# FFN gate and up kept in PSUM, and x transposed once, in a one-core hybrid decoder step

## The chip, the cores and the metric

The kernel runs on one core of a Trainium2 chip. The metric is the device time of one execution in microseconds (us). A core has five engines with a queue each, and every queue runs in order: PE (TensorE, matrix products and transposes; PEld is its weight load), DVE (VectorE), ACT (ScalarE), POOL (GpSimd) and SP, which here only issues DMAs. PE, DVE and ACT can work on PSUM, eight banks of 2 KB in each partition, into which PE writes; SBUF is the main on-chip memory.

## The reference

One inference step of a two-layer decoder, for one prompt of 512 tokens and for 8 requests of 4 tokens each, so 544 columns in all, with 1024 features. Layer 0 mixes with gated DeltaNet, layer 1 with sparse attention; each is followed by a SwiGLU FFN with 2816 hidden features. What the change touches is this part of it:

```python
def rmsnorm(x, w):
    xf = x.astype(jnp.float32)
    y = xf * lax.rsqrt(jnp.mean(xf * xf, axis=-1, keepdims=True) + NORM_EPS)
    return y.astype(x.dtype) * w

def swiglu_ffn(h, w_in, w_out):
    gate, up = jnp.split(h @ w_in, 2, axis=-1)
    return (jax.nn.silu(gate) * up) @ w_out

# run_trunk, layer l
h = rmsnorm(x, P['norm_mix'][l])
...
x = x + y
x = x + swiglu_ffn(rmsnorm(x, P['norm_ffn'][l]), P['ffn_w_in'][l], P['ffn_w_out'][l])
```

## The kernel before

Activations lie transposed: features on the 128 partitions, the 544 columns (512 prompt, 32 sample) along the free axis, in 8 blocks of 128 features. Every fp32 product is made of three matmuls: each weight tile and each activation tile is split into a rounded high part and a low part (the rest), and `gemm` (L171) issues hi*hi (L177), hi*lo (L178) and lo*hi (L179) for each of the 8 blocks. The 544 columns go in two halves, of 256 and of 288. `load_w` (L161) fetches 128 weight columns of all 8 blocks as one 128x1024 tile, ACT makes the high part `whi` (L158) and DVE, or POOL where `pool_lo` is set, the low part `wlo = wraw - whi` (L159). There are two buffers each of `whi` and `wlo`.

`start` (L227) brings x in. Five row tiles `xt` (tokens on partitions) are squared and summed, DVE and POOL make 1/rms per token in `col`, and for each half PE transposes all tiles to `raw`, which goes back to DRAM as the residual (L277, L278, L284). Then the row tiles are multiplied by their token's 1/rms (L289 on POOL, L291 on DVE), PE transposes them a second time (L300), and `make_u` (L211) takes each transposed block out of PSUM: ACT writes the high part times the norm weight `nv` (L213), DVE the low part (L214). The transposed norm weights come from one tile `vr` of 41 rows, filled by four DMAs (L294, L295). The products that follow are the decay gates (16 weight columns) and then the q, k, v projections of the DeltaNet.

`ffn` (L936) goes through 22 hidden blocks j in two groups of 11. For each j it loads a gate and an up weight tile, and for each half makes gate `pg` in a `mm` bank and up `pu` in an `aux` bank (four banks of each), 24 matmuls each. Then DVE scales gate into SBUF tile `fa` (L967), ACT takes tanh into `fth` (L968), DVE scales up into `fup` (L969), forms (1+tanh)*gate in `fth` (L970) and the hidden value in `fup` (L971), ACT rounds it to `hh` (L972), and DVE writes the rest to `hl` (L973). After 11 blocks `proj_add` multiplies by the second FFN matrix. Beside the first half of layer 0's FFN runs `past_blocks` (L1060): POOL gathers cached rows by indirect DMAs and multiplies and adds 128x512 tiles in SBUF (L1089, L1091). Layer 1's FFN has no POOL work beside it.

A scheduler puts the instructions in order on each engine when the program is built, from its own estimate of durations; on the chip each queue then runs that order.

Of the kernel before, what the change touches and what calls it, by code (L numbers as in the profile page):

```python
# [10 lines left out]
F32 = mybir.dt.float32  # L11
# [3 lines left out]
AF = mybir.ActivationFunctionType  # L15
OP = mybir.AluOpType
# [95 lines left out]
class Net:  # L112
# [114 lines left out]
    def start(self, up, hist):  # L227

        A, T, V, S, G = self.A, self.T, self.V, self.S, self.G
# [11 lines left out]
        with self.tc.tile_pool(name="xin", bufs=1) as xp:  # L241
            vr = xp.tile([48, 128], F32, name="vr")
# [9 lines left out]
            self.dma(vr[32:40], A["norm_kv"].rearrange("(k p) -> k p", p=128))  # L252
            self.dma(vr[40:41], A["dn_out_norm"])
            self.dma(cr, A["dn_conv_w"].rearrange("l i (c p) -> (l i c) p", p=128))
            self.load_consts()
            for half, (c0, cn) in enumerate(HALVES):
# [28 lines left out]
                for q in range(2):  # L285
                    for i, (t, n, _) in enumerate(tiles):
                        x = xt[t][0:n, q * 512:(q + 1) * 512]
                        if i == 1:
                            G.tensor_scalar(x, x, col[0:n, i:i + 1], 1.0, op0=OP.mult, op1=OP.mult)  # L289
                        else:  # L290
                            V.tensor_scalar(x, x, col[0:n, i:i + 1], None, op0=OP.mult)  # L291
                if half == 0:
                    ps = self.bank(next(bank))
                    T.transpose(ps[:, 0:41], vr[0:41], ident[0:41, 0:41])  # L294
                    V.tensor_copy(self.nv, ps[:, 0:41])  # L295
                    V.tensor_scalar(self.nvh, self.nv[:, 40:41], 0.5, None, op0=OP.mult)
                for k in range(KD):
                    ps = self.bank(next(bank))[:, 0:cn]
                    for t, n, o in tiles:
                        T.transpose(ps[:, o:o + n], xt[t][0:n, k * 128:(k + 1) * 128], ident[0:n, 0:n])  # L300
                    self.make_u(ps, self.nv[:, k:k + 1], *[t[:, c0:c0 + cn] for t in u[k]])

            ps = self.aux()
            T.transpose(ps[:, 0:96], cr, ident[0:96, 0:96])
            V.tensor_scalar(self.cw, ps[:, 0:96], 0.5, None, op0=OP.mult)
            for g in range(3):
# [629 lines left out]
    def ffn(self, l, u, after, side=(), steps=0):  # L936
# [5 lines left out]
        with self.tc.tile_pool(name="ffn", bufs=1) as hp, self.tc.tile_pool(name="ffs", bufs=2) as fs:  # L942
            for j0, jn in ((0, 11), (11, 11)):
                hid = []
                for j in range(j0, j0 + jn):
# [12 lines left out]
                    for c0, cn in HALVES:  # L958
# [7 lines left out]
                        a, th, up = [fs.tile([128, 288], F32, name=n)[:, :cn] for n in ("fa", "fth", "fup")]  # L966
                        V.tensor_tensor(a, pg, rstd[:, cs], op=OP.mult)  # L967
                        S.activation(th, a, AF.Tanh, scale=0.5)  # L968
                        V.scalar_tensor_tensor(up, pu, 0.5, rstd[:, cs], op0=OP.mult, op1=OP.mult)  # L969
# [847 lines left out]
```

## Time and profile before

| What | Value |
|---|---|
| median of 3 runs | 1655.19 us (1652.71 to 1656.19) |
| profiled execution | 1663.51 us |
| its span (first to last instruction) | 1661.7 us |
| mean granted TensorE clock | 0.985 of full |
| PE busy | 1598.3 us, 96% |
| DVE busy | 1062.2 us, 64% |
| ACT busy | 709.8 us, 43% |
| POOL busy | 564.5 us, 34% |

The profile is of one execution, which took 8.3 us more than the median of the runs. A busy PE in it is one with a matmul in its pipeline; a slot in which no matmul runs, or in which the granted clock is lower, lowers the count of matmuls in a stretch. In a row of a timeline the first number is the start, the second the duration, and brackets hold the engine's idle time before the instruction and who ended it. Back-to-back instructions overlap a little, so the distance of two starts is shorter than a duration.

### The profile page before, as it was taken

Reading aid. Unit: us, or ns where it says so; the run is one execution under the profiler, and the core shown is the slowest. Engines: PE = TensorE matmul, PEld = TensorE weight load, DVE = VectorE, ACT = ScalarE, POOL = GpSimd, SP = SyncE. Lnnn points to the kernel's source line nnn. Section 1 sums busy time; section 2 is a strip of 40 time slices with the busy share of each in tenths; the row PEclk is TensorE's granted clock in tenths of the full one; section 3 lists DMA queues with packets and bytes.
Section 4 is the critical chain, followed back from the end, with each engine's and each line's share of the span. In section 5 each row is a group of like instructions: output and inputs, shape, how many; then the busy total and the mean of one; then the engine's idle time right before and its main releaser. Section 6 shows DMA issues by size and latency. Waiting matters only on the chain.

```text
span 1661.7 us, 32748 instructions
## 1 busy us (share of the span) xinstructions
PE 1598.3 (96%) x12527; PEld 1528.5 (92%) x12527; DVE 1062.2 (64%) x2543; ACT 709.8 (43%) x1796; POOL 564.5 (34%) x861
## 2 busy tenths in 40 slices
PE   8998898998989999999999999999999999999997
PEld 7998788987989999999999999877999999999997
DVE  5879779487577753555556688678875553355533
ACT  5554554553323222232332487778843232132233
POOL 3675546424366711100145476565520000000000
PEclk9999999999999999999999999999999999999999
DMA  6233412257556634354342532523133332334222
GB/s 195 77 78 93 109 36 70 72 163 219 138 143 142 160 101 117 95 164 132 108 140 81 147 95 78 177 70 112 45 96 102 102 106 79 108 90 127 77 88 81
DMA packets 289069, 183.37 MB, mean 110 GB/s; under 512 B 25183, under 2 KB 271784, under 8 KB 288784
## 3 DMA queue, kind: packets, MB, share of 16 engines
q1 hardware_dynamic: 286352, 172.88, 37.5%
q0 software_dynamic: 2560, 8.39, 1.4%
q8 instruction: 99, 1.62, 0.4%
q14 instruction: 58, 0.48, 0.1%
HBM read 159.33 MB, written 26.90 MB: 112 GB/s over the span
## 4 chain that ended last, share of the span: by engine, by line
PE 77%; DVE 10%; POOL 4%; DMA 3%; ACT 3%; issue 2%; SPq 0%; POOLq 0%; DVEq 0%; ACTq 0%
PE mm L179 15%; PE mm L177 15%; PE mm L178 15%; PE aux L177 5%; PE aux L178 5%; PE aux L179 5%; PE po L1641 2%; PE aux L1668 2%; DVE hb L595 2%; DVE hb L597 1%; DVE wlo L159 1%; PE mm L1578 1%; PE mm L1579 1%; PE mm L818 1%; DVE cy L470 1%
## 5 line engine op out<-in xcount | busy, mean ns | idle before, releaser
L177 PE MATMUL mm<-uh,whi 128*128 128x288 f32 (+2 forms) x1824 | 531.3, 293 | 5.1 <-DVE hb L689 1.7
L179 PE MATMUL mm<-uh,wlo 128*128 128x288 f32 (+2 forms) x1824 | 523.8, 292 | 6.7 <-DVE wlo L159 6.7
L178 PE MATMUL mm<-ul,whi 128*128 128x288 f32 (+2 forms) x1824 | 530.1, 292 | 0.0
L158 ACT CAST whi<-wraw 128x1024 fp32r<-128x1024 f32 (+5 forms) x231 | 215.9, 936 | 524.0 <-PE mm L178 431.0
L177 PEld LDWEIGHTS mm<-uh,whi 128*128 128x128 f32 (+1 forms) x1824 | 343.9, 189 | 8.4 <-DVE hb L689 2.1
L179 PEld LDWEIGHTS mm<-uh,wlo 128*128 128x128 f32 (+1 forms) x1824 | 341.0, 189 | 9.2 <-DVE wlo L159 8.3
L178 PEld LDWEIGHTS mm<-ul,whi 128*128 128x128 f32 (+1 forms) x1824 | 344.3, 189 | 1.5 <-issue 0.4
L159 DVE TENSOR_TENSOR wlo<-wraw,whi 128x1024 fp32r<-128x1024 f32 (+5 forms) x207 | 235.5, 1138 | 118.6 <-ACT whi L158 117.2
L179 PE MATMUL aux<-uh,wlo 128*128 128x288 f32 (+1 forms) x704 | 202.7, 288 | 3.1 <-DVE wlo L159 3.1
L177 PE MATMUL aux<-uh,whi 128*128 128x288 f32 (+1 forms) x704 | 203.3, 289 | 0.0
L178 PE MATMUL aux<-ul,whi 128*128 128x288 f32 (+1 forms) x704 | 203.3, 289 | 0.0
L177 PE MATMUL mm<-hh,whi 128*128 128x256 f32 (+1 forms) x704 | 202.0, 289 | 0.0
L178 PE MATMUL mm<-hl,whi 128*128 128x256 f32 (+1 forms) x704 | 201.4, 288 | 0.0
L179 PE MATMUL mm<-hh,wlo 128*128 128x256 f32 (+1 forms) x704 | 196.5, 288 | 0.0
L179 PEld LDWEIGHTS aux<-uh,wlo 128*128 128x128 f32 x704 | 133.1, 189 | 3.6 <-DVE wlo L159 3.6
L184 POOL TENSOR_TENSOR ycol<-yvar,nhalf 128x2 f32<-128x2 f32 (+1 forms) x2 | 1.6, 775 | 390.2 <-DVE yvar L1716 390.2
L178 PEld LDWEIGHTS aux<-ul,whi 128*128 128x128 f32 x704 | 133.1, 189 | 0.0
L177 PEld LDWEIGHTS aux<-uh,whi 128*128 128x128 f32 x704 | 132.8, 189 | 0.2 <-issue 0.2
L178 PEld LDWEIGHTS mm<-hl,whi 128*128 128x128 f32 x704 | 132.6, 188 | 0.0
L177 PEld LDWEIGHTS mm<-hh,whi 128*128 128x128 f32 x704 | 132.6, 188 | 0.0
L179 PEld LDWEIGHTS mm<-hh,wlo 128*128 128x128 f32 x704 | 129.6, 188 | 0.0
L969 DVE SCALAR_TENSOR_TENSOR fup<-aux,rstd 128x256 f32<-128x256 f32 x88 | 38.6, 439 | 122.9 <-PE aux L179 122.9
(535 smaller groups left out, 2969.1 us busy)
## 6 DMA issues: line engine op xcount, KB each, us to landing
wraw<-in_ffn_w_in_dram SPq DMA_DIRECT2D x88, 512.0 KB
wraw<-in_dn_w_in_dram SPq DMA_DIRECT2D x32, 512.0 KB
wraw<-in_ffn_w_out_dram SPq DMA_DIRECT2D x32, 384.0 KB
wraw<-in_ffn_w_out_dram SPq DMA_DIRECT2D x32, 320.0 KB
hb<-in_state_dn_S_dram SPq DMA_DIRECT2D x32, 256.0 KB
wraw<-in_nsa_w_kv_dram SPq DMA_DIRECT2D x12, 512.0 KB
bskew<-bscr SPq DMA_DIRECT2D x16, 320.0 KB
x<-xd SPq DMA_DIRECT2D x16, 272.0 KB
```

The source lines that it names most:

```text
L158: self.S.copy(hi, src)
L159: (self.G if pool_lo else self.V).tensor_tensor(lo, src, hi.bitcast(F32), op=OP.subtract)
L177: self.T.matmul(ps, lhsT=hi[:, k, :], rhs=uh[:, cs], start=first and k == 0, stop=False)
L178: self.T.matmul(ps, lhsT=hi[:, k, :], rhs=ul[:, cs], start=False, stop=False)
L179: self.T.matmul(ps, lhsT=lo[:, k, :], rhs=uh[:, cs], start=False, stop=last and k == kc - 1)
L470: V.scalar_tensor_tensor(y[:, 0:SEQ], pre[:, i:i + SEQ], cw[i], y[:, 0:SEQ], op0=OP.mult, op1=OP.add)
L595: V.tensor_tensor(t, D[a][:, 0:m, l:l + 1].to_broadcast([64, m, n]), row.to_broadcast([64, m, n]), op=OP.mult)
L597: V.tensor_tensor(N[a][:, 0:m, l:32], N[a][:, 0:m, l:32], t, op=OP.subtract)
L818: T.matmul(ps, lhsT=Kh, rhs=um[q], start=True, stop=True)
L969: V.scalar_tensor_tensor(up, pu, 0.5, rstd[:, cs], op0=OP.mult, op1=OP.mult)
L1641: T.matmul(self.po, lhsT=self.VT[ty][:, kb, g], rhs=m[:, i:i + 2].rearrange("p e q -> p (e q)"), start=False, stop=last and kb > k0 and m ...
L1668: T.transpose(ps[:, i * 128:(i + 1) * 128], P[2 * pr + e][ty][:, a:a + 128], ident)
```

## The change

In `start` the second transpose is gone. 1/rms of each token is spread over all partitions by one transpose of a broadcast column (`rep`), and the block of x already transposed in `raw` (SBUF) is multiplied with it: on even blocks by one DVE instruction that also multiplies by the norm weight, followed by `split`; on odd blocks by POOL, followed by `make_u`. The norm weights needed first get a tile of their own with 32 rows; the other nine rows are transposed later. In `ffn` tanh is written into the gate's PSUM bank, up is scaled in its own bank, the product overwrites that bank, and `hh` and `hl` are made from there; only `fa` stays in SBUF. The low parts of the weights stay where they were.

```diff
-            vr = xp.tile([48, 128], F32, name="vr")
+            vr = xp.tile([32, 128], F32, name="vr")
+            vr2 = xp.tile([16, 128], F32, name="vr2")
...
-                for q in range(2):
-                    for i, (t, n, _) in enumerate(tiles):
-                        x = xt[t][0:n, q * 512:(q + 1) * 512]
-                        if i == 1:
-                            G.tensor_scalar(x, x, col[0:n, i:i + 1], 1.0, op0=OP.mult, op1=OP.mult)
-                        else:
-                            V.tensor_scalar(x, x, col[0:n, i:i + 1], None, op0=OP.mult)
                 if half == 0:
                     ps = self.bank(next(bank))
-                    T.transpose(ps[:, 0:41], vr[0:41], ident[0:41, 0:41])
-                    V.tensor_copy(self.nv, ps[:, 0:41])
-                    V.tensor_scalar(self.nvh, self.nv[:, 40:41], 0.5, None, op0=OP.mult)
+                    T.transpose(ps[:, 0:32], vr, ident[0:32, 0:32])
+                    V.tensor_copy(self.nv[:, 0:32], ps[:, 0:32])
+
+                ps = self.bank(next(bank))
+                for i, (t, n, o) in enumerate(tiles):
+                    T.transpose(ps[:, o:o + n], col[0:n, i:i + 1].to_broadcast([n, 128]), ident[0:n, 0:n])
+                rep = xp.tile([128, cn], F32, name=f"rep{half}")
+                V.tensor_copy(rep, ps[:, 0:cn])
                 for k in range(KD):
-                    ps = self.bank(next(bank))[:, 0:cn]
-                    for t, n, o in tiles:
-                        T.transpose(ps[:, o:o + n], xt[t][0:n, k * 128:(k + 1) * 128], ident[0:n, 0:n])
-                    self.make_u(ps, self.nv[:, k:k + 1], *[t[:, c0:c0 + cn] for t in u[k]])
+                    x = xp.tile([128, cn], F32, name=f"xn{half}", bufs=3)
+                    if k % 2:
+                        G.tensor_tensor(x, raw[:, k], rep, op=OP.mult)
+                        self.make_u(x, self.nv[:, k:k + 1], *[t[:, c0:c0 + cn] for t in u[k]])
+                    else:
+                        V.scalar_tensor_tensor(x, raw[:, k], self.nv[:, k:k + 1], rep, op0=OP.mult, op1=OP.mult)
+                        self.split(*[t[:, c0:c0 + cn] for t in u[k]], x)
...
-                        a, th, up = [fs.tile([128, 288], F32, name=n)[:, :cn] for n in ("fa", "fth", "fup")]
+
+                        a = fs.tile([128, 288], F32, name="fa")[:, :cn]
                         V.tensor_tensor(a, pg, rstd[:, cs], op=OP.mult)
-                        S.activation(th, a, AF.Tanh, scale=0.5)
-                        V.scalar_tensor_tensor(up, pu, 0.5, rstd[:, cs], op0=OP.mult, op1=OP.mult)
-                        V.scalar_tensor_tensor(th, th, 1.0, a, op0=OP.add, op1=OP.mult)
-                        V.tensor_tensor(up, th, up, op=OP.mult)
-                        S.copy(hh[:, cs], up)
-                        V.tensor_tensor(hl[:, cs], up, hh[:, cs].bitcast(F32), op=OP.subtract)
+                        S.activation(pg, a, AF.Tanh, scale=0.5)
+                        V.scalar_tensor_tensor(pu, pu, 0.5, rstd[:, cs], op0=OP.mult, op1=OP.mult)
+                        V.scalar_tensor_tensor(a, pg, 1.0, a, op0=OP.add, op1=OP.mult)
+                        V.tensor_tensor(pu, pu, a, op=OP.mult)
+                        S.copy(hh[:, cs], pu)
+                        V.tensor_tensor(hl[:, cs], pu, hh[:, cs].bitcast(F32), op=OP.subtract)
```

Behind `start` all engines keep the order of before, apart from a few neighbours that change places. In `start` itself the order on PE differs most. Before, the first product of the program (16 columns, the decay gates) follows the second transposes (L300) of the first half, and the second half's first transposes (L277) come behind it:

```order
L300 MATMUL ch<-ct,xt_155 128x128
L300 MATMUL ch<-ct,xt_156 128x128
L177 MATMUL mm<-uh,whi 16x256
L178 MATMUL mm<-ul,whi 16x256
L300 MATMUL ch<-ct,xt_155 128x128
L300 MATMUL ch<-ct,xt_156 128x128
L277 MATMUL aux<-ct,xt_157 128x128
```

Now it follows the transposes of both halves (L278 and L283 of the changed file), and the row of the second half's 1/rms (L293) comes right behind it:

```order
L278 MATMUL ch<-ct,xt_158 128x128
L278 MATMUL ch<-ct,xt_159 128x128
L283 MATMUL ch<-ct,xt_160 128x32 x8
L177 MATMUL mm<-uh,whi 16x256
L178 MATMUL mm<-ul,whi 16x256
L293 MATMUL aux<-ct,xcol 128x128 x2
L293 MATMUL aux<-ct,xcol 128x32
```

So PE now has all of x transposed before the first product, and ACT copies the second half's `raw` ahead of the first half's high parts. On DVE, at the same place, before: each low part is one instruction (L214) whose x operand is a PSUM bank.

```order
L187 SCALAR_TENSOR_TENSOR xcol<-rs_w,xcol 128x2
L291 TENSOR_SCALAR xt_155<-xt_155,xcol 128x512 x2
L266 SCALAR_TENSOR_TENSOR sq,xss<-xt_158 128x1024
L295 COPY nv<-ch 128x41
L270 TENSOR_SCALAR xss<-xss 128x3
L296 TENSOR_SCALAR nvh<-nv 128x1
L214 SCALAR_TENSOR_TENSOR ul<-aux,nv,uh 128x256
L214 SCALAR_TENSOR_TENSOR ul<-ch,nv,uh 128x256
```

Now (L302 is the product of an even block, L159 and L214 the low parts, `xn` the SBUF tile between):

```order
L187 SCALAR_TENSOR_TENSOR xcol<-rs_w,xcol 128x2
L267 SCALAR_TENSOR_TENSOR sq,xss<-xt_159 128x1024
L295 COPY rep_216<-aux 128x256
L302 SCALAR_TENSOR_TENSOR xn_218<-raw_184,nv,rep_216 128x256
L302 SCALAR_TENSOR_TENSOR xn_226<-raw_184,nv,rep_216 128x256
L271 TENSOR_SCALAR xss<-xss 128x3
L185 SCALAR_TENSOR_TENSOR rs_w<-xcol 128x3
L186 TENSOR_TENSOR rs_w<-rs_w,xss 128x3
L159 TENSOR_TENSOR ul<-xn_218,uh 128x256
L187 SCALAR_TENSOR_TENSOR xcol<-rs_w,xcol 128x3
L159 TENSOR_TENSOR wlo<-wraw,whi 128x8x16
L214 SCALAR_TENSOR_TENSOR ul<-xn_222,nv,uh 128x256
```

The scaling of the rows (L291) is gone, `rep` and the products came in, and both tensor operands of products and low parts are now SBUF tiles. The third place is DVE at the start of layer 0's FFN, before:

```order
L967 TENSOR_TENSOR fa<-mm,rstd 128x256
L969 SCALAR_TENSOR_TENSOR fup<-aux,rstd 128x256
L967 TENSOR_TENSOR fa<-mm,rstd 128x288
L969 SCALAR_TENSOR_TENSOR fup<-aux,rstd 128x288
L159 TENSOR_TENSOR wlo<-wraw,whi 128x1024
L970 SCALAR_TENSOR_TENSOR fth<-fth,fa 128x256
L970 SCALAR_TENSOR_TENSOR fth<-fth,fa 128x288
L971 TENSOR_TENSOR fup<-fth,fup 128x256
L967 TENSOR_TENSOR fa<-mm,rstd 128x256
L971 TENSOR_TENSOR fup<-fth,fup 128x288
L967 TENSOR_TENSOR fa<-mm,rstd 128x288
L973 TENSOR_TENSOR hl<-fup,hh 128x256
```

Now, with the lines of the changed file (L973, L975, L976, L977, L979 stand for L967, L969, L970, L971, L973 of before):

```order
L975 SCALAR_TENSOR_TENSOR aux<-aux,rstd 128x288
L159 TENSOR_TENSOR wlo<-wraw,whi 128x1024
L976 SCALAR_TENSOR_TENSOR fa<-mm,fa 128x256
L976 SCALAR_TENSOR_TENSOR fa<-mm,fa 128x288
L975 SCALAR_TENSOR_TENSOR aux<-aux,rstd 128x256
L977 TENSOR_TENSOR aux<-aux,fa 128x256
L977 TENSOR_TENSOR aux<-aux,fa 128x288
L973 TENSOR_TENSOR fa<-mm,rstd 128x256
L973 TENSOR_TENSOR fa<-mm,rstd 128x288
L979 TENSOR_TENSOR hl<-aux,hh 128x256
```

The sequence is nearly the same; what moved are operands. Each of L970, L971 and L973 had two SBUF operands and now has one operand in SBUF and one in PSUM; `wlo` still has two in SBUF.

## Rows read from the trace of the kernel before

**Rows 1.** From the page: busy time of an engine, its share of the span and its instructions.

```profile
PE 1598.3 (96%) x12527; PEld 1528.5 (92%) x12527; DVE 1062.2 (64%) x2543; ACT 709.8 (43%) x1796; POOL 564.5 (34%) x861
```

**Rows 2.** Busy time by stretch: start and end, length, then busy us (and instructions) of PE, PEld, DVE, ACT, POOL, then the granted TensorE clock, the DMA share and GB/s. The DeltaNet, the part of layer 0's FFN with POOL work beside it, and the 130 us behind it.

```profile
34.00:450.00 416.00, 391.10 (x3076) 360.46 (x3077) 317.56 (x829) 206.22 (x579) 212.99 (x326) 0.98 0.39 105
...
470.00:600.00 130.00, 122.57 (x937) 121.64 (x936) 102.80 (x126) 36.14 (x62) 81.52 (x58) 0.96 0.59 143
600.00:730.00 130.00, 130.00 (x1037) 128.95 (x1036) 59.27 (x99) 31.50 (x50) 12.35 (x8) 1.00 0.39 110
```

**Rows 3.** The same view in slices of 10 us within 470 to 600.

```profile
480.00:490.00 10.00, 9.01 (x57) 8.78 (x57) 9.96 (x10) 3.25 (x6) 9.66 (x8) 0.83 0.37 109
490.00:500.00 10.00, 8.10 (x55) 8.10 (x56) 5.73 (x9) 1.25 (x3) 2.04 (x2) 0.83 0.48 132
...
550.00:560.00 10.00, 8.14 (x53) 7.91 (x52) 9.97 (x8) 2.98 (x5) 8.86 (x8) 0.83 0.72 204
```

**Rows 4.** Timeline of PE in 470 to 600: all rows in which PE had been idle.

```profile
480.41 0.39 PE L179 MATMUL aux<-uh,wlo 128*128 128x256 f32 x1 [1.76 <-DVE wlo L159]
...
491.90 0.58 PE L179 MATMUL mm<-uh,wlo 128*128 128x256 f32 x1 [2.48 <-DVE wlo L159]
...
555.51 0.39 PE L179 MATMUL mm<-uh,wlo 128*128 128x256 f32 x1 [1.86 <-DVE wlo L159]
...
587.18 0.39 PE L179 MATMUL aux<-uh,wlo 128*128 128x256 f32 x1 [1.33 <-DVE wlo L159]
```

**Rows 5.** DVE's groups by line and shape in 450 to 600: count, busy us, mean ns of one, idle time before them.

```profile
L159 DVE TENSOR_TENSOR wlo<-wraw,whi 128x1024 fp32r<-128x1024 f32 x20 | 32.9, 1644 | 12.6 <-ACT whi L158 12.6
L973 DVE TENSOR_TENSOR hl<-fup,hh 128x256 fp32r<-128x256 f32 x11 | 13.3, 1211 | 0.0
L970 DVE SCALAR_TENSOR_TENSOR fth<-fth,fa 128x288 f32<-128x288 f32 x11 | 12.6, 1144 | 0.0
L971 DVE TENSOR_TENSOR fup<-fth,fup 128x256 f32<-128x256 f32 x11 | 10.6, 959 | 0.3
L970 DVE SCALAR_TENSOR_TENSOR fth<-fth,fa 128x256 f32<-128x256 f32 x11 | 9.9, 901 | 3.9 <-ACT fth L968 3.9
L971 DVE TENSOR_TENSOR fup<-fth,fup 128x288 f32<-128x288 f32 x11 | 8.3, 751 | 0.3
L973 DVE TENSOR_TENSOR hl<-fup,hh 128x288 fp32r<-128x288 f32 x11 | 5.7, 517 | 0.0
L967 DVE TENSOR_TENSOR fa<-mm,rstd 128x288 f32<-128x288 f32 x11 | 5.0, 451 | 1.5 <-PE mm L179 1.5
```

**Rows 6.** The same view of layer 1's FFN (1280 to 1560), where POOL does nothing.

```profile
L159 DVE TENSOR_TENSOR wlo<-wraw,whi 128x1024 fp32r<-128x1024 f32 x36 | 44.1, 1225 | 13.7 <-ACT whi L158 12.9
...
L970 DVE SCALAR_TENSOR_TENSOR fth<-fth,fa 128x256 f32<-128x256 f32 x18 | 7.7, 426 | 8.7 <-ACT fth L968 8.7
```

**Rows 7.** Timelines of DVE, ACT and POOL around the stalls at 491.90 and 555.51, and of DVE at 587.18.

```profile
486.51 2.11 DVE L971 TENSOR_TENSOR fup<-fth,fup 128x256 f32<-128x256 f32 x1
...
488.91 2.94 DVE L159 TENSOR_TENSOR wlo<-wraw,whi 128x1024 fp32r<-128x1024 f32 x1
...
485.68 1.05 ACT L158 CAST whi<-wraw 128x1024 fp32r<-128x1024 f32 x1 [1.64 <-PE mm L178]
...
551.26 4.19 DVE L159 TENSOR_TENSOR wlo<-wraw,whi 128x1024 fp32r<-128x1024 f32 x1
...
550.84 0.97 POOL L1071 DMA_INDIRECT pg<-in_cache_kv_dram,idx_cmp  x1 [0.16 <-POOL pacc L1091]
551.82 1.31 POOL L1091 TENSOR_TENSOR pacc<-pacc,ul 128x512 f32<-128x512 f32 x1
553.06 1.30 POOL L1089 TENSOR_TENSOR uh<-pg,uh 128x512 f32<-128x512 f32 x1
...
583.51 1.39 DVE L971 TENSOR_TENSOR fup<-fth,fup 128x288 f32<-128x288 f32 x1
```

**Rows 8.** Timelines of ACT, DVE and PE in the start, in this order: ACT's first high part (its last sum of squares ends as it starts), one copy of `raw`, DVE's second sum of squares, two low parts, the last low parts, and PE's first matmuls behind the decay gates.

```profile
11.95 0.45 ACT L213 ACTIVATE uh<-aux,nv 128x256 fp32r<-128x256 f32 x1
...
16.41 0.59 ACT L278 COPY raw<-aux 128x512 f32<-128x512 f32 x1
...
10.23 1.21 DVE L266 SCALAR_TENSOR_TENSOR sq<-xt 128x1024 f32<-128x1024 f32 x1
...
17.67 0.48 DVE L214 SCALAR_TENSOR_TENSOR ul<-ch,nv,uh 128x256 fp32r<-128x256 f32 x1
18.06 0.48 DVE L214 SCALAR_TENSOR_TENSOR ul<-aux,nv,uh 128x256 fp32r<-128x256 f32 x1
...
28.27 1.15 DVE L214 SCALAR_TENSOR_TENSOR ul<-ch,nv,uh 128x288 fp32r<-128x288 f32 x2 [0.58 <-ACT uh L213]
...
34.27 0.40 PE L177 MATMUL mm<-uh,whi 128*128 128x288 f32 x1
```

**Rows 9.** POOL's subtraction of a 128x1024 tile (groups by line and shape, 0 to 60), and a 128x512 product of POOL (timeline).

```profile
L159 POOL TENSOR_TENSOR wlo<-wraw,whi 128x1024 fp32r<-128x1024 f32 x2 | 4.8, 2394 | 0.0
...
501.20 1.29 POOL L1089 TENSOR_TENSOR ul<-pg,ul 128x512 f32<-128x512 f32 x1 [1.58 <-DMA ul<-in_nsa_cmp_pos_w_dram]
```

**Rows 10.** Timelines of DVE and PE where layer 0's FFN has its first 1/rms: the first scaled gate, and the first up product of the second hidden block.

```profile
466.88 0.42 DVE L967 TENSOR_TENSOR fa<-mm,rstd 128x256 f32<-128x256 f32 x1 [1.01 <-ACT rstd L207]
...
467.12 0.28 PE L177 MATMUL aux<-uh,whi 128*128 128x256 f32 x1
```

More of the change, by code (lines that the diff above doesn't have):

```diff
@@ L251, in start @@
             self.dma(xt[4][0:NS], xs)
-            self.dma(vr[32:40], A["norm_kv"].rearrange("(k p) -> k p", p=128))
-            self.dma(vr[40:41], A["dn_out_norm"])
+            self.dma(vr2[0:8], A["norm_kv"].rearrange("(k p) -> k p", p=128))
+            self.dma(vr2[8:9], A["dn_out_norm"])
             self.dma(cr, A["dn_conv_w"].rearrange("l i (c p) -> (l i c) p", p=128))
@@ L303, in start @@
             ps = self.aux()
             T.transpose(ps[:, 0:96], cr, ident[0:96, 0:96])
+            T.transpose(ps[:, 96:105], vr2[0:9], ident[0:9, 0:9])
             V.tensor_scalar(self.cw, ps[:, 0:96], 0.5, None, op0=OP.mult)
+            V.tensor_copy(self.nv[:, 32:41], ps[:, 96:105])
+            V.tensor_scalar(self.nvh, self.nv[:, 40:41], 0.5, None, op0=OP.mult)
             for g in range(3):
```

## The prediction

> **What bounds the kernel now.** I began with the page. PE is busy for 1598.3 of 1661.7 us [rows 1], so only two things can shorten the time: fewer slots without matmuls, or a PE that is released earlier. Next came the busy time by stretch. Behind 600 us PE has no gap: 1037 matmuls in 130 us. In the 130 us before, beside POOL's work, it gets through 937, at a granted clock of 0.96 [rows 2]. The missing 100 matmuls, at 130/1037 = 0.125 us each, are 12.5 us. The timeline of PE names the cause of all its idle time there: four stalls, 1.76 + 2.48 + 1.86 + 1.33 = 7.4 us, each a low weight part that DVE had not finished [rows 4]. The other 5 us are clock: three slices show a mean of 0.83 [rows 3], which is a third of each slice at the lower level of 1.2 GHz instead of 2.4, each beside or behind one of the stalls; 3 x 10 x 0.17 = 5.1 us.
>
> Why is DVE late? Its groups give the answer. Operations with both tensor operands in SBUF take long: L970, L971 and L973 have means of 517 to 1211 ns [rows 5]. In layer 1's FFN, where POOL is silent, the same L970 takes 426 ns [rows 6]. L967, which reads one operand from PSUM, takes 451 ns at the same time as POOL works [rows 5]. So an operation with two SBUF operands waits for POOL here, and one with an operand in PSUM doesn't.
>
> **The FFN edit.** Nothing is added or removed: 88 times the same seven instructions. The operands of L970, L971 and L973 move, so that each has one in PSUM. At the price of L967 and its 256-column sister (0.45 and 0.42 us) these six groups, 11 each, need 3 x 11 x 0.87 = 28.7 us in layer 0's first half. They take 13.3 + 12.6 + 10.6 + 9.9 + 8.3 + 5.7 = 60.4 us [rows 5], so about 31.7 us of DVE time go. DVE was busy for 102.8 of 130 us there [rows 2], so it becomes an engine with slack, and the 31.7 us are not the gain; the gain is bounded by the 12.5 us that PE lacks.
>
> What is late next? The low weight parts themselves: L159 keeps two SBUF operands and its mean is 1644 ns against 1225 without POOL [rows 5, 6]. So I go through the four stalls. At 587.18 the low part started only when L971 had ended, which took 1.39 us instead of 0.45 [rows 7]; that stall goes, and so does the one at 480.41, whose queue held the same operations. At 491.90 the high part was ready at 485.68 + 1.05 = 486.73, but L971 (2.11 us) stood ahead and the low part started at 488.91 [rows 7]. Started at about 487.1 and held up as long as then (2.94 us) it is ready near 490.0; PE wanted it at 491.90 - 2.48 = 489.42. About 0.6 us remain at worst. At 555.51 nothing stood ahead: the low part started at 551.26, right behind its high part, and took 4.19 us while POOL ran one gather and two sums, 0.97 + 1.31 + 1.30 [rows 7]. Moving other operations out of SBUF doesn't cure this. Its slice has 53 matmuls where 80 fit [rows 2, 3]: 27 x 0.125 = 3.4 us. POOL's bursts will not fall at the same places, so this one may vanish and another appear; I count one such stall as kept. FFN gain: 12.5 - 3.4 = 9.1 us. Upper end 12.5 (all go), lower end 3.1 (only the idle time at 480.41 and 587.18 goes, no clock).
>
> The Trainium skill (SBUF — State Buffer, "Who interferes with whom") states the rule behind these rows: a DVE instruction with two SBUF inputs contends with a GpSimd instruction that reads SBUF, one with at most one does not, and whichever comes second blocks until the first has finished. The first half agrees with 451 against 1144 ns. By the second half a low part would wait for one POOL instruction and no more; the 4.19 us row shows three passing it. By the page the FFN gain would be the full 12.5 us and the time 1640.5 us; the row decides, so I keep 9.1.
>
> In layer 1's FFN there is no POOL work and L970 is at 426 ns already [rows 6]: no gain. A gate bank is now held until L970 and an up bank until L973, some 5 us longer. A half uses one bank of each kind and PE needs 48 x 0.125 = 6 us for it; with four of each, a bank is wanted again 18 us after its product ended. Hidden, unless four banks are out at once (a rival, below).
>
> **The start.** Gone: 16 + 24 transposes (L300), 10 row scalings (L289, L291). New: 6 small transposes, two copies of `rep`, 8 products on DVE, 8 on POOL. The transposes are no gain as such: PE waits for the activations here. What counts is the end of the last low part `ul`, 28.27 + 1.15 = 29.4, and the first 128x288 matmul at 34.27 [rows 8].
>
> ACT first. Its first high part stood at 11.95 [rows 8]; now the second half's four copies of `raw` come ahead, 4 x 0.59 = 2.4 us, so 14.3. That is the loss. After it ACT has 16 high parts (0.45 to 0.50), the weights' 1.3 us and four small copies: some 10.5 us, to 24.8. DVE is the longer one. It is free at 10.23 + 1.21 = 11.4 [rows 8] and has 24 operations at about 0.41 (the distance of two L214 is 0.39, [rows 8]; 288 columns a little more) = 9.8, the weights' low parts 1.5, `rep` and `cw` 0.9, and small ones with the wait for 1/rms some 2.9 (my estimate: fourteen at 0.2): 26.5. The last block is an odd one, whose `xn` buffer comes free only with the third-last low part; its product on POOL, high part and low part (0.81 + 0.5 + 0.42) come one after the other: about 28.1.
>
> Now the other side of the FFN edit: these 24 operations read two SBUF tiles, while before L214 read PSUM. POOL's products are priced between 1.29 (512 columns) and 2.39 us (1024) [rows 9]: 2.15 ns per column more, so 0.74 and 0.81 us, 6.2 us for eight. None of it may hit (POOL waits for buffers most of the time) or all of it. I take half, as POOL has one product to three DVE operations: 31.2. The decay gates follow in 0.9 us (one copy, one transpose); the transposes of the convolution history, which stood behind the last `ul` before, stand ahead of it now. First 128x288 matmul at 32.1, a gain of 2.2 us. Ends: 29.0 (gain 5.3) and 35.2 (loss 0.9).
>
> Is a gain here carried on? From 34 to 450 us PE is busy for 391 of 416 us [rows 2] in the old order, with every engine fed by it; I count it in full.
>
> **Sum.** 9.1 + 2.2 = 11.3 us. The profiled execution would come to 1663.5 - 11.3 = 1652.2; it stands 8.3 us above the median, which should come to 1655.2 - 11.3 = 1643.9 us. By the ends: 1655.2 - 17.8 = 1637.4 and 1655.2 - 2.2 = 1653.0.
>
> **Rivals.**
> Collisions stay (0.18): POOL, no longer held up by DVE, runs its sums closer together, and the low parts lose against it more often, as at 551.26. For it: 1644 ns of L159; against it: 16 of the 20 low parts caused no stall. Gain 3.1 + 2.2: 1649.9 us.
> The start gives nothing (0.18): DVE loses all 6.2 us to POOL, as L970 did. FFN gain alone: 1646.1 us.
> Both (0.07): 3.1 - 0.9, 1653 us, hardly to be told from before.
> Slower by banks (0.04): at the start of each FFN two up banks and the two of 1/rms are out at once. If the second block's up product had to take the first block's bank, it would wait for L973 instead of L969. It is wanted at 467.12; from the first scaled gate at 466.88 [rows 10] eleven operations of 0.43, one low part of 1.22 and L973 pass: 473.4. That is 6.2 us, and 1.7 at the lower clock as behind the other stalls; in two FFNs 15.8, more than the gain: 1659.7 us. It decides as soon as banks are handed out in strict turn; against it, in the built order the second half of that product waits for ACT alone, which frees the 1/rms bank, while L973 is DVE's.
>
> **How the numbers follow.** The forecast, 1643.9 us, has 0.53, with its own range of 1640 to 1648. The range for 8 in 10 runs from 1639 to 1652: it takes in the two rivals with half a gain and leaves out the banks, most of "both" and the end where every term is best. A measurement tells about 0.2%, 3.3 us: faster means below 1651.9. Forecast 0.53, the start 0.18, collisions 0.14 of their 0.18 lie there, 0.85 in all. Within: 0.04 + 0.06 + 0.01 = 0.11. Slower: 0.04.
>
> **What would show it.** Right: L970, L971 and L973 (976, 977, 979 in the new file) at 420 to 460 ns beside POOL's sums; at most one or two stalls of PE on L159 in the FFN's first 130 us, and over 1000 matmuls there; the first 128x288 matmul near 32 us. Wrong: these operations still above 700 ns; PE idle on an L976 to L979; DVE's `ul` in the start above 1 us throughout, and the first 128x288 matmul at 34 us or later.

## The result and the profile after

The changed kernel takes 1644.83 us (median of 10 runs, 1641.46 to 1648.60), the kernel before 1655.22 beside it (10 runs, 1651.37 to 1661.04): ratio 0.9935, 95% interval 0.9918 to 0.9953, or 10.8 us faster (7.8 to 13.6). This and every other timed gain below is worked out from the ratio, which need not be that of the medians (they differ by 10.4). One execution of before_quiet, a kernel of the experiments, took 3942.93 us and counts in none of its figures. The profiled execution took 1642.95 us, span 1641.2.

The stretch of layer 0's FFN beside POOL, which had 937 matmuls at a clock of 0.96 [rows 2], is full (windows; columns as in [rows 2]):

```profile
470.00:600.00 130.00, 130.00 (x1041) 130.00 (x1040) 77.84 (x131) 37.08 (x65) 80.69 (x58) 1.00 0.60 150
```

POOL's 80.69 us are what they were (81.52); DVE fell from 102.80 to 77.84. PE has no idle time between 466 and 600. DVE's groups by line and shape in 450 to 600, to be held against [rows 5] (970, 971 and 973 are now 976, 977 and 979):

```profile
L159 DVE TENSOR_TENSOR wlo<-wraw,whi 128x1024 fp32r<-128x1024 f32 x20 | 34.8, 1739 | 14.2 <-ACT whi L158 14.1
L977 DVE TENSOR_TENSOR aux<-aux,fa 128x288 f32<-128x288 f32 x11 | 5.1, 465 | 0.3
...
L979 DVE TENSOR_TENSOR hl<-aux,hh 128x288 fp32r<-128x288 f32 x11 | 4.9, 446 | 0.0
L976 DVE SCALAR_TENSOR_TENSOR fa<-mm,fa 128x288 f32<-128x288 f32 x11 | 4.9, 445 | 0.0
L975 DVE SCALAR_TENSOR_TENSOR aux<-aux,rstd 128x256 f32<-128x256 f32 x11 | 4.8, 432 | 27.2 <-PE aux L179 27.2
L977 DVE TENSOR_TENSOR aux<-aux,fa 128x256 f32<-128x256 f32 x11 | 4.7, 431 | 0.3
L976 DVE SCALAR_TENSOR_TENSOR fa<-mm,fa 128x256 f32<-128x256 f32 x11 | 4.7, 423 | 3.7 <-ACT mm L974 3.6
...
L979 DVE TENSOR_TENSOR hl<-aux,hh 128x256 fp32r<-128x256 f32 x11 | 4.5, 413 | 0.0
```

The six groups need 413 to 465 ns instead of 517 to 1211. The low parts, which keep two SBUF operands, are no shorter (1739 ns), but they start sooner: in this stretch a 128x1024 one starts at most 0.56 us behind the end of its high part, and before it was up to 5.58 us. Most of DVE's idle time now stands ahead of L975, where it waits for PE (27.2 us).

The start, from the timelines of DVE (its second sum of squares and its last low part), PE, ACT and POOL, against [rows 8]:

```profile
9.73 1.22 DVE L267 SCALAR_TENSOR_TENSOR sq<-xt 128x1024 f32<-128x1024 f32 x1 [0.18 <-DMA xt<-in_x_prompt_dram]
...
28.98 0.52 DVE L214 SCALAR_TENSOR_TENSOR ul<-xn,nv,uh 128x288 fp32r<-128x288 f32 x1 [1.27 <-ACT uh L213]
...
30.23 0.40 PE L177 MATMUL mm<-uh,whi 128*128 128x288 f32 x1
...
32.09 0.21 ACT L402 ACTIVATE hv<-hv 128x8 f32<-128x8 f32 x1 [2.15 <-DMA hv<-in_dn_A_log_dram]
...
33.59 2.36 POOL L159 TENSOR_TENSOR wlo<-wraw,whi 128x1024 fp32r<-128x1024 f32 x1 [3.49 <-ACT whi L158]
...
36.00 0.47 PE L179 MATMUL mm<-uh,wlo 128*128 128x256 f32 x1 [1.24 <-POOL wlo L159]
```

The last low part ends at 29.5, and the first 128x288 matmul is at 30.23 instead of 34.27. In part that is this execution. DVE's second sum of squares stands ahead of the chain and waits for its rows of x to land; it starts between 9.73 (here) and 11.57 in the traces. Counted from there, the matmul comes 20.4 to 20.7 us later in the six traces with this start (the changed kernel, and start_only, hv_early, start_small, after_small and hv_small below), and 23.4 to 24.5 us later in the seven with the old one. So the start gains 3 to 4 us at this point.

Then ACT waits 2.15 us for the decay constants `hv`. Their tile lies in memory that the start's pool frees, so its loads are issued only at 29.56, when the last low part has ended. The high part behind that wait is late, so is its low part on POOL, and PE stands idle until 36.00. The windows behind the stall show the granted clock (last but two) near the 1.2 GHz level, half of 2.4:

```profile
36.00:38.00 2.00, 2.00 (x10) 2.00 (x11) 1.97 (x5) 0.98 (x3) 1.84 (x4) 0.54 0.33 51
38.00:40.00 2.00, 2.00 (x13) 2.00 (x12) 2.00 (x6) 0.00 (x0) 1.84 (x3) 0.61 0.97 271
```

Where PE stands over the whole execution I read by matching each matmul with the same one in the trace of before; the table has the difference of their starts in us (minus: earlier), by the time in before. It is worked out from the traces and is no view of the profile.

```
time in before   40     58    190    300    440    480    605   1000   1100   1600
after          -1.22  -0.88  +0.98  +1.49  -0.30  -0.58 -13.62 -13.93 -18.52 -20.56
ffn_only       +0.46  +0.46  +2.32  +2.33  +1.49  +3.61  -8.20  -7.83 -12.63 -14.14
start_only     -1.62  -0.63  -0.97  -0.98  -2.66  +0.48  -3.10  -3.45  -8.70  -8.98
hv_early       -2.45  -2.44  -1.94  -2.16  -3.99  -0.79  -6.50  -6.07 -11.20 -11.97
start_dve      -1.41  -1.39  +0.13  +0.16  -1.99  +1.40 -11.64 -10.58 -16.51 -17.03
before_small   +0.32  +0.32  -0.08  -0.11  -0.10  -2.07 -15.11 -15.33 -14.81 -14.65
after_small    -0.55  -0.53  -0.41  -0.24  -0.99  -2.97 -16.01 -15.40 -15.01 -15.34
```

In the changed kernel the FFN gives 13.04 us (from 480 to 605). The start's 4.0 us are 0.9 at 58 us, and between 140 and 190 another 1.9 are lost; ffn_only, whose code ahead of the FFN is that of before, loses 1.9 us in the same place, so this loss is not the start's. Another 4.6 to 5.9 us between 1000 and 1100 appear in all five kernels above before_small, start_only and ffn_only among them, though nothing was changed in that stage: the profiled execution of before was slow there (it stands 8.3 us above its median), and so were those of before_small and after_small, for a reason that was not followed. The profiles' difference, 20.6 us, is therefore not the effect of the change; the timed 10.8 is.

### The profile page after: what moved, and what is told of

The parts are those of the page before. It is cut to its first block, busy times and chain, and to the rows that moved or that the text cites. A ratio compares the mean times of both kernels' runs of the same rounds, so it can differ in the third digit from the quotient of the medians.

```text
span 1641.2 us, 32685 instructions
## 1 busy us (share of the span) xinstructions
PE 1585.5 (97%) x12493; PEld 1520.5 (93%) x12493; DVE 1036.1 (63%) x2548; ACT 703.3 (43%) x1796; POOL 568.4 (35%) x865
## 4 chain that ended last, share of the span: by engine, by line
PE 79%; DVE 9%; DMA 4%; POOL 3%; issue 2%; ACT 2%; SPq 1%; POOLq 0%; DVEq 0%; ACTq 0%
PE mm L179 15%; PE mm L177 15%; PE mm L178 15%; PE aux L177 5%; PE aux L178 5%; PE aux L179 5%; PE po L1647 3%; DVE hb L600 2%; PE aux L1674 2%; DVE hb L602 2%; PE mm L1584 1%; SPq L155 1%; PE mm L1585 1%; PE mm L823 1%; DVE cy L475 1%
## 5 line engine op out<-in xcount | busy, mean ns | idle before, releaser
L159 DVE TENSOR_TENSOR wlo<-wraw,whi 128x1024 fp32r<-128x1024 f32 (+5 forms) x207 | 237.7, 1149 | 121.7 <-ACT whi L158 120.5
L975 DVE SCALAR_TENSOR_TENSOR aux<-aux,rstd 128x256 f32<-128x256 f32 x88 | 39.4, 448 | 139.0 <-PE aux L179 138.9
```

The costliest lines, as they stand in the source:

```text
L159: (self.G if pool_lo else self.V).tensor_tensor(lo, src, hi.bitcast(F32), op=OP.subtract)
L975: V.scalar_tensor_tensor(pu, pu, 0.5, rstd[:, cs], op0=OP.mult, op1=OP.mult)
```

## The experiments

The twelve kernels ran on three chips, four on each. The kernel before took 1656.21, 1656.27 and 1660.48 us there, so kernels of different chips are compared by their ratios only.

| kernel | median us (range) | before on that chip | ratio (95%) |
|---|---|---|---|
| ffn_only | 1648.11 (1645.73–1651.05) | 1656.21 | 0.9954 (0.9938–0.9970) |
| start_only | 1652.32 (1648.33–1657.15) | 1656.21 | 0.9968 (0.9952–0.9983) |
| before_quiet | 1659.62 (1655.66–1662.76) | 1656.21 | 1.0025 (1.0010–1.0039) |
| ffn_quiet | 1660.51 (1657.55–1661.91) | 1656.21 | 1.0024 (1.0011–1.0036) |
| tanh_psum | 1653.39 (1647.37–1656.24) | 1656.27 | 0.9978 (0.9962–0.9994) |
| up_psum | 1652.02 (1645.81–1657.52) | 1656.27 | 0.9983 (0.9965–1.0001) |
| hv_early | 1645.08 (1642.15–1653.37) | 1656.27 | 0.9938 (0.9915–0.9960) |
| start_dve | 1644.48 (1640.92–1646.54) | 1656.27 | 0.9930 (0.9907–0.9954) |
| before_small | 1648.31 (1647.56–1649.58) | 1660.48 | 0.9926 (0.9900–0.9953) |
| start_small | 1648.12 (1643.48–1649.65) | 1660.48 | 0.9921 (0.9894–0.9949) |
| after_small | 1648.86 (1648.08–1649.41) | 1660.48 | 0.9930 (0.9904–0.9956) |
| hv_small | 1646.66 (1646.25–1647.64) | 1660.48 | 0.9917 (0.9891–0.9943) |

**ffn_only.** The kernel before with the seven lines of the FFN as in the change, nothing else.

> The kernel before with the FFN's edit alone. Theory (the FFN's DVE operations waited for POOL because both of their operands lay in SBUF, and the low weight parts behind them came late): between 470 and 600 us PE runs through, about 1040 matmuls instead of 937 at a granted clock near 1, L970, L971 and L973 at 420 to 460 ns, and the time falls by 10 to 13 us, to about 1643 us (ratio 0.993). Rival (the time came from the new start): at most 2 us below the kernel before, with the four stalls of PE still there.

It is 7.6 us faster (5.0 to 10.3), less than the 10 to 13 expected, though its trace gains 11.8 us in the FFN and the six groups stand at 414 to 465 ns. It reaches the FFN 3.6 us late (the table at 480): 1.5 of these it has at 440 already, and 2.1 come from a collision just ahead of the FFN (timelines of POOL, DVE and PE):

```profile
458.19 0.98 POOL L1071 DMA_INDIRECT pg<-in_cache_kv_dram,idx_cmp  x1
459.02 3.76 DVE L159 TENSOR_TENSOR wlo<-wraw,whi 128x1024 fp32r<-128x1024 f32 x1 [9.62 <-ACT whi L158]
459.19 1.29 POOL L1091 TENSOR_TENSOR pacc<-pacc,uh 128x512 f32<-128x512 f32 x1
460.42 1.27 POOL L1091 TENSOR_TENSOR pacc<-pacc,ul 128x512 f32<-128x512 f32 x1
461.85 1.77 POOL L1071 DMA_INDIRECT pg<-in_cache_kv_dram,idx_cmp  x1 [0.16 <-issue]
...
462.84 0.39 PE L179 MATMUL mm<-uh,wlo 128*128 128x256 f32 x1 [2.77 <-DVE wlo L159]
```

This is the last low part of the DeltaNet's output projection. It started while a gather ran, and did not get through until POOL paused at 461.69 for 0.16 us; PE waited 2.77 us, and its clock fell to 0.83 in the next 10 us. By the matched matmuls that costs 4.1 us. Of these 2.0 come back, because PE then has no wait for the FFN's 1/rms. In the kernel before the same low part came first, and that wait is there:

```profile
457.53 1.23 DVE L159 TENSOR_TENSOR wlo<-wraw,whi 128x1024 fp32r<-128x1024 f32 x1 [9.62 <-ACT whi L158]
...
457.75 1.87 POOL L1071 DMA_INDIRECT pg<-in_cache_kv_dram,idx_cmp  x1
...
465.40 0.24 PE L204 MATMUL aux<-ct,rcol 32*128 32x32 f32 x1 [1.87 <-DVE rcol L187]
```

Here it took 1.23 us, and the gather, 0.22 us later, was the one held up (1.87 instead of 0.98). start_only, hv_early and start_dve lost here too (3.87 to 4.26 us for the low part; 5.1 to 5.3 us, of which 1.9 to 2.0 come back), up_psum and the changed kernel did not. This place was in nobody's sum, because before had no stall there.

**start_only.** The changed kernel with the FFN's seven lines as before.

> The changed kernel with the FFN's edit undone, so the new start alone. Theory (the 4.0 us by which the first 128x288 matmul comes earlier are lost again before the first FFN, as the changed kernel's trace shows 0.6 us left at 465 us): first 128x288 matmul near 30.2 us, some 937 to 960 matmuls in the FFN's first 130 us as before, and 0 to 1 us below the kernel before (ratio 0.9995 to 1.0). Rival (the start's gain is carried on, as the prediction counted it): 2 to 4 us below, ratio 0.9975 to 0.9985.

The rival's number is nearer: 5.3 us faster (2.8 to 7.9). But the trace doesn't show these as carried from the start: it is 0.63 us ahead at 58 us. Its FFN then loses 9.5 of the 13.04 us rather than all, with three stalls on L159 (492.82, 554.91, 582.57) in place of the four of [rows 4]:

```profile
470.00:600.00 130.00, 124.67 (x966) 123.81 (x965) 103.20 (x129) 36.63 (x63) 82.84 (x57) 0.97 0.58 145
```

So a start that moves PE by a few us also moves which low parts meet POOL. One profile can't tell how much of the 5.3 us (the medians differ by 3.9) is that; before_small and start_small below take the collisions away.

**before_quiet and ffn_quiet.** POOL's products and sums of the compressed blocks left out behind the first row, without and with the FFN's edit:

```diff
-                t = w[i] if r else acc[:, i]
-                G.tensor_tensor(t, g, w[i], op=OP.mult)
-                if r:
-                    G.tensor_tensor(acc[:, i], acc[:, i], t, op=OP.add)
+                if r == 0:
+                    G.tensor_tensor(acc[:, i], g, w[i], op=OP.mult)
```

> The kernel before, without POOL's products and sums on the rows behind the first of each compressed block (these sums hold only their first row; gathers and loads stay): POOL is nearly silent in layer 0's FFN, the FFN's operands stay in SBUF. Theory (POOL's sums are what makes L970, L971 and L973 long): these operations at 420 to 460 ns, no stall of PE on L159, about 1040 matmuls in 470 to 600 us, and some 12 us below the kernel before (ratio about 0.993) without any edit of the FFN; if POOL's sums also cost something elsewhere, more. Rival (the operands' place counts by itself, or the hidden-unit chain is late for another reason): the four stalls stay and the time is within 3 us of the kernel before.

> As before_quiet (the same products and sums of the compressed blocks left out), with the FFN's edit. Theory (the edit's whole worth is that it keeps clear of POOL): within 2 us of before_quiet. Rival (operands in PSUM are faster by themselves, or the edit shortens the queue in another way): about 10 us below before_quiet, or at least 4.

The FFN did what the theory says: no stall on L159 behind 480 us, and 13.04 us gained there by both kernels, with and without the edit. The totals agree with each other as expected (1.0025 and 1.0024). Against the kernel before they are 4 us slower, the opposite of what was expected, and that is no measure of POOL: leaving instructions out changed the planned order. A sum of squares that DVE needs now stood on POOL behind the gathers (DVE's timeline, and PE's):

```profile
457.49 2.69 DVE L224 TENSOR_TENSOR acc<-acc,sq 128x256 f32<-128x256 f32 x1 [14.24 <-POOL acc L224]
...
461.73 0.58 PE L179 MATMUL aux<-uh,wlo 128*128 128x256 f32 x1 [13.37 <-DVE wlo L159]
```

As an experiment on the total this failed; before_small does it with the order unchanged.

**tanh_psum and up_psum.** One half of the edit each.

```diff
 tanh_psum:
-                        S.activation(th, a, AF.Tanh, scale=0.5)
+                        S.activation(pg, a, AF.Tanh, scale=0.5)
...
-                        V.scalar_tensor_tensor(th, th, 1.0, a, op0=OP.add, op1=OP.mult)
+                        V.scalar_tensor_tensor(a, pg, 1.0, a, op0=OP.add, op1=OP.mult)
 up_psum:
-                        V.scalar_tensor_tensor(up, pu, 0.5, rstd[:, cs], op0=OP.mult, op1=OP.mult)
+                        V.scalar_tensor_tensor(pu, pu, 0.5, rstd[:, cs], op0=OP.mult, op1=OP.mult)
...
-                        V.tensor_tensor(up, th, up, op=OP.mult)
+                        V.tensor_tensor(pu, pu, th, op=OP.mult)
```

> The kernel before, with only the tanh written into the gate's bank, so that of the three long DVE operations L970 alone gets an operand in PSUM; product and hidden value stay in SBUF. Theory (only an operation with two SBUF operands waits for POOL): L970 at 420 to 450 ns between 465 and 600 us, L971 and L973 still at 500 to 1200 ns; DVE's excess falls by 12.9 of 31.7 us, and PE keeps some of its stalls on L159: 970 to 1010 matmuls in 470 to 600 us, 3 to 8 us below the kernel before. Rival (it is the load of DVE as a whole that counts, and any relief ends the stalls): over 1030 matmuls and the full gain of ffn_only, 7.6 us.

> The kernel before, with only the up product and the hidden value kept in their bank, so that L971 and L973 get an operand in PSUM and L970 keeps two in SBUF. Theory: L971 and L973 at 410 to 470 ns, L970 still at 900 ns or more; DVE's excess falls by 18.8 of 31.7 us; most stalls go, more than with tanh_psum, since L971 and L973 stand directly ahead of the low parts: 1000 to 1040 matmuls in 470 to 600 us, 5 to 9 us below the kernel before. Rival (L970 takes over the time that the others lose, since POOL's work is the same): L970 above 1500 ns and a gain below 3 us.

Each operation follows its own operands. DVE's groups of tanh_psum, 465 to 600 us:

```profile
L973 DVE TENSOR_TENSOR hl<-fup,hh 128x256 fp32r<-128x256 f32 x11 | 12.2, 1113 | 0.0
L971 DVE TENSOR_TENSOR fup<-fup,fa 128x256 f32<-128x256 f32 x11 | 8.8, 803 | 0.3
...
L970 DVE SCALAR_TENSOR_TENSOR fa<-mm,fa 128x288 f32<-128x288 f32 x11 | 4.9, 445 | 0.0
```

and of up_psum:

```profile
L970 DVE SCALAR_TENSOR_TENSOR fth<-fth,fa 128x288 f32<-128x288 f32 x11 | 13.7, 1243 | 0.0
...
L973 DVE TENSOR_TENSOR hl<-aux,hh 128x288 fp32r<-128x288 f32 x11 | 4.9, 445 | 0.0
```

Matmuls in 470 to 600 us are 997 and 1034, both within the theory's bounds. In time, 3.6 and 2.8 us, the two can't be told apart; up_psum's runs spread over 11.7 us, its interval reaches no change, and the 5 to 9 us expected of it were not confirmed. In the traces the FFN gains 9.0 and 12.1 of the 13.04 us (480 to 605), in the expected order; tanh_psum's execution lost another 4.9 us ahead of the FFN, where PE waited for POOL's step of the 1/rms.

**hv_early.** The changed kernel with the `hv` tile in a pool of its own:

```diff
+            for i, nm in enumerate(("dn_A_log", "dn_dt_bias")):
+                self.dma(self.hv[:, i], ...)
...
+        self.hv = dn.tile([128, 2, 8], F32, name="hv")
```

> The changed kernel, with the tile of the decay constants in a pool of its own and its two loads issued at the start, behind that of the convolution weights. Theory (the 4 us won at 34 us are lost at 36 us, because the loads of that tile can be issued only when the start's pool is free, and ACT waits for them ahead of the weights' high parts): no wait of ACT on the decay constants, no stall of PE on a low part at 36 us, and PE 2.5 to 4 us ahead of the kernel before at 58 us, where the changed kernel is 0.9 ahead. If that is carried on, 2 to 3 us below the changed kernel, about 1642 us, ratio to before 0.9915 to 0.992. Rival (what is won here is swallowed by the waits of the next stage, or by the clock): within 1 us of the changed kernel.

The theory of the stall holds: no wait of ACT for `hv`, no stall at 36 us, a clock of 1.00 there, and PE 2.44 us ahead at 58 and 4 ahead at 440 us (the changed kernel 0.9 and 0.3). The time is the same as that of the changed kernel within the interval, so the rival's figure came. The profiled execution shows one way to lose it: the low part ahead of the FFN (3.87 us), and then in the FFN the longest of all runs:

```profile
542.24 1.31 POOL L1098 TENSOR_TENSOR pacc<-pacc,ul 128x512 f32<-128x512 f32 x1
542.45 7.10 DVE L159 TENSOR_TENSOR wlo<-wraw,whi 128x1024 fp32r<-128x1024 f32 x1 [0.54 <-ACT whi L158]
...
543.50 1.30 POOL L1096 TENSOR_TENSOR uh<-pg,uh 128x512 f32<-128x512 f32 x1
...
544.75 1.28 POOL L1096 TENSOR_TENSOR ul<-pg,ul 128x512 f32<-128x512 f32 x1
545.98 1.26 POOL L1098 TENSOR_TENSOR pacc<-pacc,uh 128x512 f32<-128x512 f32 x1
547.20 1.25 POOL L1098 TENSOR_TENSOR pacc<-pacc,ul 128x512 f32<-128x512 f32 x1
548.61 1.80 POOL L1078 DMA_INDIRECT pg<-in_cache_kv_dram,idx_cmp  x1 [0.16 <-issue]
...
549.60 0.58 PE L179 MATMUL mm<-uh,wlo 128*128 128x256 f32 x1 [4.50 <-DVE wlo L159]
```

Five POOL instructions without a gap pass the low part. It runs in the first gap, at 548.45, and now the gather is the one that waits. PE loses 4.50 us and a clock step.

**start_dve.** The changed kernel with `if False:` for `if k % 2:`, so that DVE makes all 16 products.

> The changed kernel, with all 16 products of the start on DVE and none on POOL. Theory (half of POOL's 6.2 us of products is paid by DVE as waiting, the other half hidden, so that moving eight products of 0.4 us to DVE costs what it saves): no operation of DVE in 10 to 29 us held up (products and low parts at 0.4 to 0.5 us each), first 128x288 matmul between 29.5 and 31 us, and the time within 1.5 us of the changed kernel. Rival (POOL's contention costs more than the products): first 128x288 matmul before 29 us and PE more than 2 us ahead of the kernel before at 58 us.

None is held up, as the theory has it: DVE's products take 480 and 513 ns, its low parts 419 and 452. The last low part ends at 29.52, as in the changed kernel (29.50), but here the second sum of squares started 1.24 us later, at 10.97. From there the chain is 1.2 us shorter, so in these two traces POOL's share cost about 1.2 us more than eight products on DVE. The time, from 4 runs, can't be told from that of the changed kernel. (The first 128x288 matmul is at 32.98 because PE took other products first; it is 1.4 us ahead at 58 us, so the rival's 2 us are not reached.)

**before_small, start_small, after_small, hv_small.** Every instruction in its old place, but POOL's products and sums of the compressed blocks cover 16 of 512 columns behind the first row:

```diff
-                G.tensor_tensor(t, g, w[i], op=OP.mult)
+                n = 16 if r else 512; G.tensor_tensor(t[:, 0:n], g[:, 0:n], w[i][:, 0:n], op=OP.mult)
...
-                    G.tensor_tensor(acc[:, i], acc[:, i], t, op=OP.add)
+                    G.tensor_tensor(acc[:, i, 0:n], acc[:, i, 0:n], t[:, 0:n], op=OP.add)
```

> The kernel before with its instructions in the old order on every engine, but POOL's 60 products and sums of the compressed blocks behind the first two cover 16 of 512 columns (so these sums are left out for the other columns). Theory (all that the FFN's edit wins is POOL's hold on SBUF): PE without a stall on L159 between 440 and 600 us, L970, L971 and L973 at 410 to 460 ns, and 9 to 14 us below the kernel before, as much as or more than the FFN's edit alone (7.6), since the low part ahead of the FFN, near 457 us, can't be held up either. Rival (the quiet POOL gains less than the edit, so that the edit has a worth of its own): less than 6 us below the kernel before.

> before_small with the new start, so the FFN's edit undone and the same columns of POOL's products and sums left out. It tells what the start is worth where POOL's sums can hold up nothing behind it. Theory (of the 4 us at 34 us, the late decay constants take back three, and 0.6 to 1 us is carried): 0 to 1.5 us below before_small. Rival (the 5.3 us by which start_only was timed faster are the start's own): 3 to 6 us below before_small.

> start_small with the FFN's edit: the changed kernel with the same columns of POOL's products and sums left out. Theory: within 1 us of start_small, since the edit only keeps DVE clear of POOL; and below the changed kernel by what POOL's hold still costs there, 2 to 5 us, with its times closer together than the changed kernel's two groups (1641 to 1643 and 1646 to 1649), if these come from the low part near 457 us. Rival (the operands' place has a worth of its own): 4 us or more below start_small.

> after_small with the tile of the decay constants loaded at the start, as in hv_early. Theory (PE is 1.6 us further ahead at 58 us, and this is carried on where no collision with POOL swallows it): 1 to 2.5 us below after_small. Rival (swallowed by the stages behind or by the clock): within 0.7 us of after_small.

before_small is 12.3 us faster than before (7.8 to 16.6) without any edit of the FFN. In its trace the FFN gains the same 13.04 us, and 2.0 more come ahead of it, since the wait for the 1/rms is gone too. Its window, and its L970 and L973 with both operands in SBUF:

```profile
470.00:600.00 130.00, 130.00 (x1041) 130.00 (x1040) 68.47 (x126) 37.16 (x63) 27.47 (x55) 1.00 0.64 151
```

```profile
L970 DVE SCALAR_TENSOR_TENSOR fth<-fth,fa 128x288 f32<-128x288 f32 x11 | 4.9, 450 | 0.0
L973 DVE TENSOR_TENSOR hl<-fup,hh 128x256 fp32r<-128x256 f32 x11 | 4.7, 428 | 0.0
```

With POOL quiet the edit is worth nothing: after_small is 0.7 us above start_small. The start is worth 0.2 us by the medians (1648.31 to 1648.12), with a spread of 6.2 us in start_small; its trace is 1.4 us ahead of before_small at 58 us, level at 396 and 0.2 behind at the end. With `hv` early the time falls by 2.2 us, and the two ranges do not touch: the expected 1 to 2.5 us, carried to the end once POOL can't swallow them. The spread falls as well: on the same chip before ranges over 12.9 us (11 runs), before_small over 2.0 (6 runs), after_small over 1.3 (start_small over 6.2, for one run at 1643.48). That after_small would be 2 to 5 us below the changed kernel did not show: their ratios are 0.9930 and 0.9935, on different chips. In the traces after_small is 1.5 us ahead of the changed kernel at 1000 us and 5.2 behind at 1600, so what was missing lies in the stage behind 1000, which stays open.

## Why the prediction was right, and where it wasn't

Forecast 1643.9, measured 1644.83; 11.3 us against 10.8. The main reason is shown. The two terms are not what I had put down: the FFN alone was timed at 7.6 us, and the start at 5.3 with POOL's collisions or 0.2 without, which makes 12.9 or 7.8. That the sum came within half a microsecond is luck.

**What bounds the FFN: shown.** Its idle slots came from DVE's two-SBUF operations beside POOL. Take POOL's columns away, or take the operands out of SBUF: either way the FFN gains the same 13.04 us in the traces, and together no more, since PE then has no idle time left there. The signs that I named for it are there: 413 to 465 ns (420 to 460 forecast), over 1000 matmuls, at most two stalls.

**The FFN's term, 9.1 us: right in size, by luck of one execution.** Alone it measures 7.6 (5.0 to 10.3). The step "I count one such stall as kept", 3.4 us, stood for a low part like the one at 555.51 [rows 7]. That low part met POOL in two of the four full edits profiled: 0 us in the changed kernel and start_dve, a stall of 0.93 us in ffn_only, 4.50 in hv_early. So the rival "collisions stay" described something real, and it is not the outcome of every execution. Its price was bounded by a 4.19 us low part; 7.10 was seen. I also took the 4.19 us row for the rule, and it is the exception (last section). Two things were missed. First, a collision just ahead of the window, near 457 us, that costs 4.1 to 5.3 us where it falls, 2.1 to 3.4 after what comes back. Second, the 12.5 us were read from one execution that stands 8.3 us above the median and taken off the median; start_only's trace, with the same FFN, loses 9.5 where before's loses 13.04.

**The start's term, 2.2 us: a chain 1.2 us too long, and one step that failed.** The last low part, forecast at 31.2, ended at 29.5. From DVE's being free it took 18.6 us (10.88 to 29.50) instead of 19.8. The small operations with the wait for 1/rms took 2.0 us instead of the 2.9 that I had estimated, and the 23 products and low parts ahead of the last 9.0 without POOL's hits instead of 9.4; the hits cost DVE 3.4 us, close to the 3.1 assumed. The other 0.5 us is x, which landed earlier in this execution than in that of before. In four of the other five traces with this start it landed later, and the first 128x288 matmul is at 31.64 to 32.10; that these lie so near the forecast 32.1 is chance. The step that failed is "I count it in full". The gates followed within 0.73 us, but the stage behind them waited for `hv`, whose loads I had not followed past the pool: 4.0 us became 0.9. With POOL quiet the start is worth about 0.2 us, so "the start gives nothing" (1646.1) was the better account of this term, though not for its reason: DVE did not lose all 6.2 us to POOL. The 5.3 us of start_only are not explained by this; that they are shifted collisions fits its trace but was not shown.

**Banks: fell.** PE has no idle time between 466 and 600 us, nor in layer 1's FFN (1280 to 1560).

**Which version is best** stays open: start_dve and hv_early measure like the changed kernel, and only with POOL's columns left out does hv early show its 2.2 us.

## What to carry to other kernels

Before a stall's idle time is booked as a gain, look at how far the profiled execution lies from the median, and at the instructions that just missed a collision: a low part 0.22 us ahead of a gather is a stall in the next version. When an earlier finish is booked, follow the first instruction behind it on every engine to its loads, and to the pool whose release lets them be issued; and see how early the chain's first load landed in that execution. To test contention, shrink the other engine's instructions in place and keep the order; leaving them out replans the program.

## What the runs showed of the hardware

An operation of DVE with two SBUF operands and a POOL instruction held each other up, and the one that came second waited, on either side. In most cases it waited for one instruction, as in the changed kernel ahead of the FFN (timelines of POOL and DVE):

```profile
457.99 1.60 POOL L1097 TENSOR_TENSOR pacc<-pacc,uh 128x512 f32<-128x512 f32 x1
458.51 2.17 DVE L159 TENSOR_TENSOR wlo<-wraw,whi 128x1024 fp32r<-128x1024 f32 x1
459.56 2.27 POOL L1097 TENSOR_TENSOR pacc<-pacc,ul 128x512 f32<-128x512 f32 x1
```

The low part got in behind the sum that ran when it came, though the next sum stood right behind; that one was then held, 2.27 us instead of 1.29. Counted over the 128x1024 low parts between 450 and 600 us in the eight traces with POOL's full columns (before, changed, ffn_only, start_only, hv_early, start_dve, tanh_psum, up_psum): 93 took over 1.4 us. 86 of them came while a sum or product ran, and 83 of these ended 1.08 to 1.09 us behind the end of that one instruction. The other three let one to four more pass (7.10 us in hv_early is the longest). The remaining seven, among them the low parts of 3.76 and 4.19 us, came in the last 0.66 us of a gather, and were passed by the one or two sums or products right behind it. With the full edit, each stall of PE on a low part of over 0.3 us in that stretch (five, in ffn_only, hv_early and start_dve) stands behind one of these ten.

So the Trainium skill (SBUF — State Buffer, "Who interferes with whom") is borne out in who is affected (with a PSUM operand, 413 to 465 ns beside POOL), and in most cases in that the second blocks until the first has finished; the ten waited longer, and why is open.

A PSUM operand cost nothing here: 288 columns of the tanh product took 450 ns from SBUF (before_small) and 448 from PSUM (after_small):

```profile
L976 DVE SCALAR_TENSOR_TENSOR fa<-mm,fa 128x288 f32<-128x288 f32 x11 | 4.9, 448 | 0.0
```

With POOL's columns cut, the spread of the times on one chip fell from 12.9 us (11 runs) to 2.0 (6 runs), which fits the collisions as its main source; the 6.2 us of start_small, from one early run, are not explained.
